# Down projection in seven block products over 16 of 22 key tiles, with the sums of weight blocks made earlier by GpSimd

## The chip, the core and the metric

The kernel runs on one core of a Trainium2 chip. The metric is device time in microseconds (us) of one execution. Engines are called by the profile's names: PE (TensorE matmuls), PEld (its weight loads), DVE (VectorE), ACT (ScalarE), POOL (GpSimd) and SP (SyncE, which here issues nearly all transfers, in one queue in order).

## The reference, cut to what matters

One encoder layer over 1024 tokens of width 1024: a token mixer (mLSTM heads and neighbourhood attention behind one input projection), a cross attention into 256 memory tokens, and a gated feed-forward part with a depthwise convolution, each followed by a layer norm of `alpha * x + f(x)`. Two of its parts matter here: the last matrix product `y @ w_down`, with 22 x 128 = 2816 hidden columns, and the projection of the normed input, out of which the q and k of the mLSTM heads come.

```python
def conv_ffn(x, w_up, b_up, w_dw, b_dw, w_down, b_down):
    h = x @ w_up + b_up
    h = lax.conv_general_dilated(h, w_dw[:, None, :], window_strides=(1,), padding='SAME', ...) + b_dw
    g, u = jnp.split(h, 2, axis=-1)
    y = jax.nn.gelu(g, approximate=False) * u
    return y @ w_down + b_down
...
    z = x @ w_in + b_in                      # in hybrid_mixer: q, k, v, gates, ... of both head groups
...
    h = layer_norm(DN_ALPHA * h + conv_ffn(h, w_up[l], b_up[l], w_dw[l], b_dw[l], w_down[l], b_down[l]),
                   ln3_w[l], ln3_b[l])
```

## The kernel before

All large products are made of f16 pairs: an f32 operand, scaled by a power of two, is split into a high part (ACT, line 203) and a low part (DVE, line 204; both in `split16`), and `mm3` (lines 224 to 226) issues three matmuls, high by high, high by low, low by high. The scale comes from a bound on the operand: an ACT pass with `Abs` and an accumulated sum for weights, then a maximum over partitions by way of TensorE (`amax_all`, lines 182 and 183, tile `mx`) and a few small DVE operations (`pow2`, 174 to 176).

The program is written with a tile scheduler, which sorts the instructions of each engine by a timeline that it simulates itself; `tc.issue_after(x)` keeps an instruction behind another. A tile of a pool with n buffers waits until the last readers of the one n before it are done. Each engine, and SP's queue of transfers, then works strictly in the order so found.

Stages, with rough times in the trace: the memory's keys and values and the input projections (to 254); the q/k units (254 to 340), four blocks of weights by a seven-product scheme (`units_gen`, `cu_prep`: two 512 KB loads at line 458 into `wraw` (two buffers), bounds at 310, splits, four GpSimd sums at 476 to 479, splits of the sums; each product is 48 matmuls of 128x512 in tile `cu`); behind the 14th product `back_gen` (mLSTM state) runs beside them; then mLSTM, column projections, neighbourhood attention, cross attention; the feed-forward loop (850 to 1205), 22 units of seven products each (tile `z`) with the convolution on ACT and DVE and the gated product `y` stored tile by tile to DRAM (`y_d`, line 1715). Beside the loop, `survey_down` loads each of the 22 tiles of `w_down` (512 KB, tile `sv`) and takes its bound on ACT.

The down projection begins inside the last two units: `y_scale(0)` gives the scale of y for the key tiles below `NG` = 18 (the last four have a scale of their own). `y_pair` loads two key tiles of y (1 MB) into one of three rotating raw buffers (`raw8`: two called `two`, one `ur`) and splits them; `w_pair` loads `w_down` by 512 KB into `wraw` and splits it. `dmm` runs `mm3` over key tiles for one of eight token tiles and one of two column halves of 512, in bank tile `dn`. The first column half goes over all token tiles and is kept in `half0`; the second is made token tile by token tile, and each is followed by its norm (`ln_tile`, lines 239 to 258: statistics and products on DVE, a power step on POOL at line 244, a scaling on ACT, an add on POOL at 258) and its store. The residual row `r` is loaded from DRAM (line 1922) and scaled by two POOL passes of 128x1024 (lines 1929 and 1930).

## Time and profile before

| What | Value |
|---|---|
| median of 3 runs | 1470.32 us (1469.87 to 1471.45) |
| profiled execution, its own time | 1471.42 us |
| its span (first to last instruction) | 1469.6 us |
| mean granted TensorE clock | 0.991 |
| busy: PE / DVE / ACT / POOL | 98% / 70% / 56% / 38% |
| matmuls of tile `dn` by line 224, 225 and 226, largest groups | 105 us busy each, no idle time before them |
| transfers | 208.60 MB, mean 142 GB/s |

The span is cut into stretches below: for each engine its busy time. An instruction's row has its start and length in us, the engine, the line (of a helper where one issued it), the operation, what it writes and reads, and in brackets how long its engine had been idle and which instruction released it. A group's row has count, total busy time and mean ns of one, then idle time before and its releasers. Matmuls overlap: their interval is read from one start to the next, not from the length of one.

### The profile page before, as it was taken

What the parts mean: (1) busy time and instruction counts of PE and PEld (TensorE: products, weight loads), DVE (VectorE), ACT (ScalarE), POOL (GpSimd) and SP (SyncE); (2) the same over time, 40 slices, a digit from 0 to 9 for tenths busy, and PEclk for the clock granted to TensorE, in tenths of its full rate; (3) what the DMA queues carried; (4) which work ended last, traced back from release to release, by engine and by line L of the source; (5) the groups of instructions that cost most, each with busy time, mean ns of one, the idle gap of its engine ahead of it and who ended that gap; (6) DMA issues with size and microseconds to landing.
All of it is one profiled execution on the core that took longest, in us unless ns stands there. A gap on an engine that the chain in (4) does not pass through costs nothing.

```text
span 1469.6 us, 21479 instructions
## 1 busy us (share of the span) xinstructions
PE 1435.0 (98%) x7996; PEld 847.4 (58%) x7996; DVE 1031.0 (70%) x1950; ACT 821.9 (56%) x1385; POOL 559.5 (38%) x440
## 2 busy tenths in 40 slices
PE   8999899999999999999999999999999999999998
PEld 6998777456766777774444444444444444444445
DVE  7877866536767787689657778878887879627333
ACT  5765465665454476524455678787777667411010
POOL 4452356502233765145214053544444400302352
PEclk9999999999999999999999999999999999999999
DMA  8855654213554643653443333333334228621111
GB/s 305 308 192 185 188 196 152 94 50 116 162 140 149 222 143 123 245 181 78 92 100 101 118 109 130 146 117 127 117 129 149 96 99 289 228 84 46 58 58 58
DMA packets 116382, 208.60 MB, mean 142 GB/s; under 512 B 40627, under 2 KB 69555, under 8 KB 112950
## 3 DMA queue, kind: packets, MB, share of 16 engines
q1 hardware_dynamic: 115984, 206.47, 42.2%
q8 instruction: 63, 1.03, 0.3%
q0 software_dynamic: 144, 0.49, 0.2%
q14 instruction: 41, 0.34, 0.1%
q10 hardware_dynamic: 150, 0.27, 0.0%
HBM read 154.15 MB, written 45.15 MB: 136 GB/s over the span
## 4 chain that ended last, share of the span: by engine, by line
PE 78%; DVE 7%; DMA 5%; ACT 4%; issue 3%; POOL 2%; SPq 1%; DVEq 0%; ACTq 0%; POOLq 0%
PE z L226 7%; PE z L225 7%; PE z L224 7%; PE dn L224 5%; PE dn L226 5%; PE dn L225 5%; PE S L224 4%; PE S L225 4%; PE S L226 4%; PE tk L225 2%; PE tk L224 2%; PE tk L226 2%; PE cl L224 2%; PE cl L225 2%; PE cl L226 2%
## 5 line engine op out<-in xcount | busy, mean ns | idle before, releaser
L225 PE MATMUL dn<-wlo,yp 128*128 128x512 f16 (+1 forms) x284 | 105.1, 370 | 0.0
L224 PE MATMUL dn<-whi,yp 128*128 128x512 f16 (+1 forms) x284 | 105.0, 370 | 0.0
L226 PE MATMUL dn<-whi,yp 128*128 128x512 f16 (+1 forms) x284 | 104.3, 370 | 0.0
L1708 DVE SCALAR_TENSOR_TENSOR cbuf<-C,wdw,cbuf 128x1024 f32<-128x1024 f32 x44 | 64.9, 1477 | 39.3 <-ACT cbuf L1707 39.3
L226 PEld LDWEIGHTS <-wlo 128*128 128x128 f16 x540 | 52.8, 98 | 56.7 <-DVE wlo L204 1.5
L224 PEld LDWEIGHTS <-whi 128*128 128x128 f16 x540 | 52.8, 98 | 56.1 <-issue 3.2
L225 PEld LDWEIGHTS <-whi 128*128 128x128 f16 x540 | 52.8, 98 | 54.5 <-issue 1.8
L244 POOL TENSOR_TENSOR lnrs<-lnrs,mhalf 128x1 f32<-128x1 f32 x32 | 23.4, 731 | 154.9 <-DVE lnrs L243 148.1
L1566 POOL TENSOR_TENSOR wraw<-two 128x512 f32<-128x512 f32 x15 | 30.1, 2009 | 123.0 <-issue 121.8
L204 DVE SCALAR_TENSOR_TENSOR wlo<-wraw,us,whi 128x1024 f16<-128x1024 f32 (+1 forms) x48 | 61.7, 1305 | 18.6 <-ACT whi L203 18.6
L1709 DVE SCALAR_TENSOR_TENSOR cbuf<-C,wdw,cbuf 128x1024 f32<-128x1024 f32 x44 | 71.3, 1622 | 1.1
L1707 ACT ACTIVATE cbuf<-C,bdw,wdw 128x1024 f32<-128x1024 f32 x44 | 54.2, 1237 | 18.4 <-DVE C L1745 17.7
L203 ACT ACTIVATE whi<-wraw,us 128x1024 f16<-128x1024 f32 (+1 forms) x48 | 51.0, 1103 | 15.3 <-DVE us L176 14.7
L224 PEld LDWEIGHTS <-yp 128*128 128x128 f16 x370 | 36.2, 98 | 39.9
L225 PEld LDWEIGHTS <-yp 128*128 128x128 f16 x370 | 36.2, 98 | 39.8
L226 PEld LDWEIGHTS <-yp 128*128 128x128 f16 x370 | 36.2, 98 | 39.7
L254 ACT ACTIVATE r<-r,lnrs 128x1024 f32<-128x1024 f32 x11 | 13.6, 1238 | 79.3 <-DVE lnrs L253 79.2
L224 PE MATMUL tk<-whi,Bo 128*128 128x256 f16 (+1 forms) x192 | 53.2, 277 | 1.6 <-DVE stage L204 1.6
L224 PE MATMUL tk<-whi,Be 128*128 128x256 f16 (+1 forms) x192 | 52.6, 274 | 0.9 <-DVE stage L204 0.9
L225 PE MATMUL tk<-wlo,Be 128*128 128x256 f16 (+1 forms) x192 | 52.4, 274 | 0.9 <-DVE wlo L204 0.9
L225 PE MATMUL tk<-wlo,Bo 128*128 128x256 f16 (+1 forms) x192 | 53.2, 277 | 0.0
L226 PE MATMUL tk<-whi,Bo 128*128 128x256 f16 (+1 forms) x192 | 53.1, 277 | 0.0
(556 smaller groups left out, 4854.2 us busy)
## 6 DMA issues: line engine op xcount, KB each, us to landing
two<-in_w_up_dram SPq DMA_DIRECT2D x15, 1024.0 KB
sv<-in_w_down_dram SPq DMA_DIRECT2D x22, 512.0 KB
y<-cbuf SPq DMA_DIRECT2D x22, 512.0 KB
wraw<-in_w_down_dram SPq DMA_DIRECT2D x22, 512.0 KB
ur<-in_w_up_dram SPq DMA_DIRECT2D x7, 1024.0 KB
two<-y SPq DMA_DIRECT2D x7, 1024.0 KB
r<-h SPq DMA_DIRECT2D x11, 512.0 KB
wraw<-in_w_tok_dram SPq DMA_DIRECT2D x10, 512.0 KB
```

The costliest lines, as they stand in the source:

```text
L203: A.activation(hi, src, AF.Copy, scale=s)
L204: return V.scalar_tensor_tensor(lo, src, s, hi, op0=OP.mult, op1=OP.subtract)
L224: T.matmul(ps, lh, rh, start=first, stop=False, skip_group_check=skip)
L225: T.matmul(ps, lh, rl, start=False, stop=False, skip_group_check=skip)
L226: return T.matmul(ps, ll, rh, start=False, stop=last, skip_group_check=skip)
L244: G.tensor_tensor(rs[:, 0:1], rs[:, 0:1], mhalf[:, 0:1], OP.pow)
L254: A.activation(r, r, AF.Identity, scale=rs[:, 0:1], bias=rs[:, 1:2])
L1566: G.tensor_tensor(S1, A21, A22, OP.add)
L1707: A.activation(c, C[:, 1:SEQ + 1], AF.Identity, scale=wdw[:, 1, j:j + 1], bias=bdw[:, j:j + 1])
L1708: V.scalar_tensor_tensor(c, C[:, 0:SEQ], wdw[:, 0, j:j + 1], c, op0=OP.mult, op1=OP.add)
L1709: V.scalar_tensor_tensor(c, C[:, 2:SEQ + 2], wdw[:, 2, j:j + 1], c, op0=OP.mult, op1=OP.add)
```

## The change

The down projection takes the key tiles 0 to 15 as 2 x 2 blocks: two halves of the tokens, two halves of the keys (eight tiles each), two halves of the columns. It forms seven products instead of eight: A11B11, A12B21, A22T4, and with sums of blocks n2T2, n1T1, s3T3, n4B22; each is four token tiles by eight key tiles by three matmuls of 128x512. `a_sums` makes the sums of y blocks in the stage (two DVE and two POOL operations of 128x512 for each of eight steps). The products are gathered in `C`, eight tiles of 128x1024, by `into` (ACT copies, DVE adds). The six key tiles 16 to 21 (`NG` = 16) go in a last pass, token tile by token tile, both column halves, each followed by its norm; `rest(n)` has prepared the residual in three POOL passes. All splits of y and `w_down` are made in this stage, from raw buffers of 128x2048 by `raw8`.

The sums of weight blocks T1 to T4 are made beside the q/k units by `td_gen`, in 16 steps at every 1st, 3rd, 5th and 7th product of a unit: a 512 KB load into `draw` (three buffers), the bound by ACT `Abs`, four POOL additions in place, a 512 KB store to `td_d` in DRAM. `survey_down` in the feed-forward loop is left with six of its 22 loads and ACT passes.

```diff
+            def td_gen():
+                ...
+                load(0)
+                load(1)
+                for n in range(16):
+                    raw = raws.pop(n)
+                    with tc.issue_after(taken[0].ins):
+                        A.activation(junk, raw.rearrange("p b c -> p (b c)"), AF.Abs, accum_out=sums[:, NFF + n:NFF + n + 1])
+                    B11, B12, B21, B22 = (raw[:, i] for i in range(4))
+                    G.tensor_tensor(B11, B11, B12, OP.add)
+                    G.tensor_tensor(B12, B12, B22, OP.add)
+                    G.tensor_tensor(B22, B22, B11, OP.add)
+                    G.tensor_tensor(B21, B21, B22, OP.add)
+                    o = n // 2 * 512 + n % 2 * 256
+                    S.dma_start(td_d[:, :, o:o + 256].rearrange("n p c -> p n c"), raw)
+                    load(n + 2)
+                    yield
...
             for n, _ in enumerate(units_gen(cu0)):
+                if n % 7 % 2 == 0:
+                    next(td, None)
                 if n >= 14:
                     next(bg, None)
+            run(td)
             run(bg)
...
-        NG = NFF - 4
+        NG = 16
...
+            def a_sums(i, s):
+                ...
+                V.tensor_tensor(t[:, 0], o, o8, OP.subtract)
+                V.tensor_tensor(t[:, 1], t[:, 0], e, OP.subtract)
+                G.tensor_tensor(u[:, 0], e, o, OP.subtract)
+                G.tensor_tensor(u[:, 1], t[:, 1], e8, OP.add)
+                for m, src in enumerate((t, u)):
+                    h = SH[m][i // 4][:, :, :, i % 4]
+                    split16(h[:, 0], h[:, 1], src, s)
...
+            def b_form(name, home):
+                ...
+                for q in range(2):
+                    raw = raw8()
+                    if name[0] == "B":
+                        S.dma_start(raw.rearrange("p (i c) -> p i c", i=4),
+                                    I["w_dn"][4 * q:4 * q + 4, :, n * 512:n * 512 + 512].rearrange("i p c -> p i c"))
+                    else:
+                        S.dma_start(raw, td_d[n, :, q * 2048:q * 2048 + 2048])
+                    h, l = home[q]
+                    split16(h, l, raw, sd)
...
+            def dprod(banks, a, b, first, js=range(4), outer=False):
+                for j, i in [(j, i) for i in range(8) for j in js] if outer else [(j, i) for j in js for i in range(8)]:
+                    t = slice(j * 128, j * 128 + 128)
+                    h, l = a[i]
+                    mm3(banks[j], h[:, t], l[:, t], *BF_[b][i], first and i == 0, i == 7, skip=True)
...
+            b_form("B11" ...); a_plain("A11" ...); b_form("B21" ...); a_plain("A12" ...); b_form("T4" ...); a_plain("A22" ...)
+            dprod(Z4, A12, "B21", True)
+            b_form("T2", kept["H0"])
+            for i in range(4):
+                a_sums(i, s1)
+            dprod(Z4, A22, "T4", True)
+            b_form("T1", YH)
+            for i in range(4, 8):
+                a_sums(i, s1)
+            dprod(X4, n2, "T2", False, outer=True)
+            b_form("T3", H1)
+            dprod(W4, n1, "T1", True, outer=True)
+            b_form("B22", kept["H0"])
+            dprod(X4, s3, "T3", False, outer=True)
+            order = [4, 5, 6, 7, 0, 1, 2, 3]
+            def rest(n):
+                tt, r = order[n], wp.tile([128, WP], F32, name="wraw", tag="wraw", bufs=2)[:, :D]
+                S.dma_start(r, h2_d[tt * 128:(tt + 1) * 128, :])
                 G.tensor_tensor(r, r, rw, OP.mult)
                 G.tensor_tensor(r, r, rb, OP.add)
+                G.tensor_tensor(C[tt], C[tt], r, OP.add)
...
+            for tt in order:
+                r = C[tt]
+                for a, n in ((0, 512), (512, 256), (768, 256)) if last else ((0, 512), (512, 512)):
+                    p = bank("dn")[:, :n]
+                    for f in range(NG, NFF):
+                        mm3(p, ys[f][0][:, t0], ys[f][1][:, t0], wl[f][0][:, a:a + n], wl[f][1][:, a:a + n], ...)
+                    V.scalar_tensor_tensor(r[:, a:a + n], p, ratio, r[:, a:a + n], op0=OP.mult, op1=OP.add)
                 ln_tile(r, lw, lb, small, late=last, eps=ep, parts=2 if last else 1, pieces=4 if last else 2)
```

Lines of the changed file are higher by one from line 200 on, and more from 990 on. The order shows the rest. SP's queue at the third and fourth q/k unit, before: the loads of `w_cu` (the last two are the fourth unit's) follow one another.

```order
L828 DMA mo<-ev 128x256 x3
L930 DMA mo<-mo 128x512 x2
L458 DMA wraw<-in_w_cu_dram 128x1024 x4
L916 DMA whi<-mrow 128x512 x2
L948 DMA wraw<-in_w_col_dram 128x1024
```

And now:

```order
L931 DMA mo<-mo 128x512 x2
L459 DMA wraw<-in_w_cu_dram 128x1024 x2
L1006 DMA td<-draw 128x4x256
L991 DMA draw<-in_w_dn_dram 128x4x256
L1006 DMA td<-draw 128x4x256 x2
L991 DMA draw<-in_w_dn_dram 128x4x256
L459 DMA wraw<-in_w_cu_dram 128x1024
L991 DMA draw<-in_w_dn_dram 128x4x256
L459 DMA wraw<-in_w_cu_dram 128x1024
L1006 DMA td<-draw 128x4x256
L991 DMA draw<-in_w_dn_dram 128x4x256
```

Three stores of sums (`td<-draw`, of steps 0 to 2) and four loads of `draw` now stand ahead of the last `w_cu` load; the load in the last row is that of step 6, behind the store of step 3. The first three `draw` loads stand far ahead, in the 13th place of SP's queue at the program's start.

ACT at the split of the fourth unit, before:

```order
L310 ACTIVATE whi,l_3511<-wraw 128x1024
L505 ACTIVATE q_3217<-cu,bsc,us 128x2x128
L505 ACTIVATE q_3219<-cu,bsc,us 128x2x128
L505 ACTIVATE k_3218<-cu,bsc,us 128x2x128
L505 ACTIVATE k_3220<-cu,bsc,us 128x2x128
L203 ACTIVATE whi<-wraw,us 128x512
L203 ACTIVATE whi<-wraw,us 128x1024
L203 ACTIVATE whi<-ev_3620,us 128x512
```

And now:

```order
L311 ACTIVATE whi,l_3584<-wraw 128x1024
L506 ACTIVATE q_3218<-cu,bsc,us 128x2x128
L506 ACTIVATE q_3220<-cu,bsc,us 128x2x128
L999 ACTIVATE djunk,sums<-draw 128x1024
L506 ACTIVATE k_3219<-cu,bsc,us 128x2x128
L506 ACTIVATE k_3221<-cu,bsc,us 128x2x128
L204 ACTIVATE whi<-wraw,us 128x512
L999 ACTIVATE djunk,sums<-draw 128x1024
L204 ACTIVATE whi<-wraw,us 128x1024
L204 ACTIVATE whi<-ev_3709,us 128x512
```

The bound of step 5 (first L999) stands ahead of the unit's split, that of step 6 (second L999) between its first two pieces.

POOL beside the last token tiles' norms, now (`lnrs` is the power step of a norm, `L259` the last add of a norm, `L2010` to `L2012` the passes of `rest`):

```order
L245 TENSOR_TENSOR lnrs<-lnrs,mhalf 128x1
L2010 TENSOR_TENSOR wraw<-wraw,vec_12595 128x1024 x2
L2011 TENSOR_TENSOR wraw<-wraw,vec_12597 128x1024
L259 TENSOR_TENSOR D_12146<-D_12146,ur 128x1024
L2011 TENSOR_TENSOR wraw<-wraw,vec_12597 128x1024
L245 TENSOR_TENSOR lnrs<-lnrs,mhalf 128x1
L2012 TENSOR_TENSOR D_12144<-D_12144,wraw 128x1024
L2012 TENSOR_TENSOR D_12145<-D_12145,wraw 128x1024
L245 TENSOR_TENSOR lnrs<-lnrs,mhalf 128x1
```

Four passes of `rest` and one add stand between the first tile's power step and the second's, two more passes ahead of the third's. Before, two passes of 128x1024 and one add stood between one tile's power step and the next one's.

242 lines of the change are left out of this document (128 added, 114 removed).

## The prediction

> **What bounds the kernel now.** I read the busy shares first, then the windows of the stages that the change touches, then the waits there, and the chain of waits last.
>
> ```profile
> PE 1435.0 (98%) x7996; PEld 847.4 (58%) x7996; DVE 1031.0 (70%) x1950; ACT 821.9 (56%) x1385; POOL 559.5 (38%) x440
> PE 78%; DVE 7%; DMA 5%; ACT 4%; issue 3%; POOL 2%; SPq 1%; DVEq 0%; ACTq 0%; POOLq 0%
> ```
>
> ```profile
> 250.00:300.00 50.00, 48.33 (x247) 24.35 (x245) 29.08 (x64) 30.64 (x56) 22.15 (x19) 1.00 0.32 110
> 300.00:350.00 50.00, 49.12 (x290) 30.62 (x289) 23.80 (x71) 33.87 (x90) 8.11 (x9) 1.00 0.35 96
> 1000.00:1050.00 50.00, 50.00 (x235) 22.73 (x234) 40.01 (x47) 38.21 (x48) 23.67 (x12) 1.00 0.34 127
> 1200.00:1250.00 50.00, 50.00 (x235) 23.03 (x234) 44.84 (x51) 39.48 (x44) 0.00 (x0) 1.00 0.68 228
> 1300.00:1350.00 50.00, 50.00 (x234) 22.84 (x233) 28.20 (x34) 8.64 (x8) 10.18 (x4) 1.00 0.19 64
> 1400.00:1450.00 50.00, 50.00 (x234) 22.65 (x232) 18.55 (x33) 3.72 (x3) 21.08 (x11) 1.00 0.17 64
> ```
>
> The columns after the window's length are busy time (and count) of PE, its weight loads, DVE, ACT, POOL, then the granted clock, the DMA share and GB/s. In the feed-forward loop (1000) and in the down projection (1205 to 1462) TensorE is busy for all 50 us of each window at full clock: a matmul less there is its whole interval less. In the q/k units it lacks 1.7 and 0.9 us of 50, so it is nearly the bound there too, but with something close behind it. Their first product and the last start at:
>
> ```profile
> 253.83 0.38 PE L224 MATMUL cu<-Be,whi 128*128 128x512 f16 x1
> 337.98 0.38 PE L224 MATMUL cu<-TX1h,whi 128*128 128x512 f16 x1
> ```
>
> **The change, part by part.**
>
> *Fewer products.* Before, 8 token tiles x 22 key tiles x 2 column halves x 3 matmuls = 1056 of 128x512. Now 7 products x 96 = 672, and 8 x 6 x 2 x 3 = 288 for the six tiles left, 960 together. The interval:
>
> ```profile
> 1099.79 0.38 PE L226 MATMUL z<-TX1l,unitYl 128*128 128x512 f16 x1
> 1101.08 0.38 PE L226 MATMUL z<-TX1l,unitYl 128*128 128x512 f16 x1
> ```
>
> Six matmuls take 1.29 us, 0.215 each (the windows' 234 in 50 us say 0.214): 96 x 0.215 = **-20.6 us**, if TensorE stays dense.
>
> *Whether it stays dense.* The stage takes in 34 transfers of 1 MB into three rotating raw buffers, where 11 such and 22 of half the size stood before, and splits all but the eight of the row sums at the full 128x2048. The prices:
>
> ```profile
> 1205.55 2.19 ACT L203 ACTIVATE yp<-two,sc 128x1024 f16<-128x1024 f32 x2 [2.19 <-DVE sc L176]
> L203 ACT ACTIVATE yp<-two,sc 128x1024 f16<-128x1024 f32 x14 | 15.2, 1137 | 9.6 <-DVE sc L176 9.0 <-PE z L226 0.7
> L204 DVE SCALAR_TENSOR_TENSOR yp<-two,sc,yp 128x1024 f16<-128x1024 f32 x14 | 17.5, 1280 | 0.2 <-ACT yp L203 0.2
> L938 DVE TENSOR_TENSOR whi<-whi,G 128x512 f32<-128x512 f32 x16 | 10.2, 678 | 0.0
> L1932 DVE TENSOR_TENSOR r<-r,half 128x512 f32<-128x512 f32 x4 | 5.1, 1275 | 1.8 <-POOL r L1930 1.8
> 1370.97 0.34 SPq L1945 DMA_DIRECT2D out_dram<-r  x1
> 1373.65 0.32 SPq L1922 DMA_DIRECT2D r<-h  x1
> 1377.11 2.36 POOL L1929 TENSOR_TENSOR r<-r,vec 128x1024 f32<-128x1024 f32 x1 [6.17 <-DMA r<-h]
> ```
>
> A raw is split in 2 x 1.14 us on ACT and 2 x 1.28 on DVE behind it. DVE's sum over the seven products (151 us of TensorE): 34 x 2.56 = 87, two subtractions for each of eight row sums = 11, sixteen adds of bank halves = 11, 109 together, 72%. So DVE has room. A buffer's round is its load, then the split, about 3.8 until DVE is done. 512 KB need 3.46 us from issue to use (1373.65 to 1377.11); at the 228 GB/s of the window at 1200 another 512 KB adds 2.3, so 5.8 + 3.8 = 9.6 us, and 34 such in three buffers are 109 us, again under 151. I cost the density at 0; the cover is this difference of some 42 us, and if it is gone TensorE waits for the overhang (a rival below). The first split waits, as before, for the scale (at 1205.55), and TensorE has the last unit's products to do meanwhile.
>
> *The end.* GpSimd now does three passes of 128x1024 for each token tile (two before), the last twelve of them in its queue among the last tiles' norms, and each row load waits for one of two buffers.
>
> ```profile
> L1930 POOL TENSOR_TENSOR r<-r,vec 128x1024 f32<-128x1024 f32 x4 | 11.3, 2844 | 0.1
> L258 POOL TENSOR_TENSOR wraw<-wraw,yp 128x1024 f32<-128x1024 f32 x3 | 7.4, 2475 | 7.7 <-DVE wraw L257 7.7
> L1941 DVE TENSOR_TENSOR r<-r,dn 128x512 f32<-128x512 f32 x4 | 2.8, 689 | 26.6 <-PE dn L226 26.6
> 1462.37 0.43 DVE wraw L1941
> ```
>
> A token tile's matmuls now come every 36 x 0.215 = 7.8 us. The second tile's power step stands behind five of these passes (5 x 2.5 = 12 us) plus a load of 3.5, so I estimate it some 7 us late. DVE waits there in order, and a tile costs it about 5 us, so it catches up about 2.8 us on each of six tiles. Best case 0; worst, nothing caught up: 7. I take **+2.5**, nearer to the catching up. What follows the last matmul stays about 7.5 us (1462 to 1469.6).
>
> *Weight sums beside the q/k units.* Sixteen steps: one ACT pass (1.06 + 0.19, as in the rows at 287.71 and 288.68), four GpSimd adds of 128x256, a store, a load. GpSimd was 30 us busy in these 100 (the first two windows), DMA 0.33: by totals, 16 x 4 x 0.67 = 43 us of GpSimd and 16 MB fit. What doesn't is the order. The rows of before around the fourth unit:
>
> ```profile
> 281.21 1.90 SPq L458 DMA_DIRECT2D wraw<-in_w_cu_dram  x2
> 287.71 1.06 ACT L310 ACTIVATE whi<-wraw 128x1024 bf16<-128x1024 f32 x1
> 288.68 0.19 ACT L310 ACTIVATION_READ_ACCUMULATOR whi<-wraw 128x1 f32 x1
> 287.76 1.27 POOL L476 TENSOR_TENSOR ev<-wraw 128x512 f32<-128x512 f32 x1 [1.26 <-DMA wraw<-in_w_cu_dram]
> 298.29 0.29 DVE L183 TENSOR_REDUCE us<-mx 128x1 f32<-128x128 f32 x1 [1.86 <-PE mx L182]
> 299.18 1.76 ACT L203 ACTIVATE whi<-wraw,us 128x512 f16<-128x512 f32 x2
> 300.85 1.32 ACT L203 ACTIVATE whi<-ev,us 128x512 f16<-128x512 f32 x2
> PE cu L226 <- DVE wlo L204: 0.8, 1, 0.8
> 290.00:300.00 10.00, 10.00 (x50) 4.86 (x48) 3.57 (x12) 1.84 (x4) 1.65 (x2) 1.00 0.07 23
> L736 POOL TENSOR_TENSOR tsum<-Bo 128x256 f32<-128x256 f16 x8 | 5.4, 674 | 0.0
> L739 POOL TENSOR_TENSOR tsum<-Bo,tsum 128x256 f32<-128x256 f16 x8 | 7.6, 946 | 0.0
> ```
>
> Its last two weight loads are issued at 281 to 283 and are there at 285.0 and 287.7; now stores of three steps' sums, each waiting for GpSimd, stand ahead of them in SP's queue, so I put them at about 290. That alone is harmless, since the split waits for the maximum at 298.3. But the ACT pass of step 6 now stands between the first piece of that split (299.18) and the rest, and it needs a load that waits for the third step's store to have landed, whose last add stands on GpSimd behind the fourth unit's own four adds. GpSimd from 290: four of 1.27 and five of 0.67 to 0.95, about 9.2, is 299; the store 2.7 (1370.97 to 1373.65, from a store to the load that reuses its buffer), the load 3.46, the pass 1.25: 306.6, against 299.9 before for that piece. TensorE had no slack there (it waited 0.8 us for this split), so it stops some 7 us; best case 4 (loads on time), worst 12. A stop brings the half clock:
>
> ```profile
> 25.55 1.09 PE L612 MATMUL tp<-ident,x 128*128 128x128 f32 x8 [0.29 <-POOL x L258]
> 30.13 0.58 PE L226 MATMUL mem<-memTh,wlo 128*128 128x256 f32 x1 [3.49 <-DVE wlo L577]
> 36.27 0.33 PE L224 MATMUL mem<-memTh,whi 128*128 128x256 f32 x1
> ```
>
> After 3.5 us idle the intervals are half speed from 30.1 to 36.3, which loses 3.1 us. At other places it may be shorter, so I take 2 to 3: **+9** in all (0 if the order does not bite, 15). By the Trainium skill, "TensorE: Matmul & The Clock Gate", Part 1, full clock returns after about 3.4 us of sustained work. That would make the loss 1.7 us and the sum 1 us lower; the row's 6.1 us of half clock says more. After this step the chain goes on at 11 to 12 us for each buffer's round, and ends about with the shifted units, so I add nothing.
>
> *The start.* The first three loads of the sums (1.5 MB) have no producer and stand 13th in SP's queue, among the loads of the first 25 us.
>
> ```profile
> 5.00:15.00 10.00, 10.00 (x26) 6.12 (x25) 7.91 (x9) 7.80 (x9) 3.11 (x1) 1.00 1.02 408
> 15.00:25.00 10.00, 10.00 (x84) 10.00 (x83) 8.88 (x20) 4.50 (x7) 5.41 (x4) 1.00 1.03 413
> ```
>
> DMA is full there: 1.5 MB at 410 GB/s are 3.8 us for whatever stands behind. TensorE already waits for weights at 30, but that wait ends on splits, not on a load. I take **+1.5**, between -1 (another order) and +5.
>
> *The loop.* Sixteen ACT passes of 1.2 us and 8 MB of loads leave the feed-forward loop: TensorE is dense there at ACT 38 of 50, so 0.
>
> Sum: -20.6 + 2.5 + 9 + 1.5 = **-7.6 us**. The profiled execution took 1471.42 us with a span of 1469.6, which makes a span of 1462.0 and a time of 1463.8; the median run, 1470.32, is 1.1 us below the profiled one, so **1462.7 us**.
>
> **Rivals.**
>
> *The sums ride free.* If the fourth unit's loads keep their place and step 6 comes in time, the +9 is gone: 1453.7. For it: GpSimd is busy only 1.65 us between 290 and 300, so the third step's adds have room if they come ahead of the unit's own. Against: store, load and pass follow the last of these adds by 7.4 us, so it must be done by 292.5, some 2.5 us after the loads at 290.
>
> *The sums set the pace* (the slower side). Sixteen steps through three buffers are 5.3 rounds; the 84 us between the units' first product and their last allow 15.8 us a round. My round is 1.24 + 2.7 to 3.8 + 2.7 + 3.46 = 10 to 11 us alone. From 15.8 on, each ACT pass holds ACT's queue, and the units with it. At 19 us a round the units take 101 us, +17 more in place of the catch-up and beside the one stop: -20.6 + 2.5 + 17 + 9 + 1.5 = +9.4, 1479.7. It ends slower than before once a round is over 17.3 us. For it: an add waits on GpSimd behind units' adds, and a pass on ACT behind splits. Against: GpSimd is under half full.
>
> *The down stage starves.* A buffer's round over 151 x 3 / 34 = 13.3 us makes the raws the bound. DVE operations with two inputs beside GpSimd take 1.28 us where 0.68 is normal (the L1932 row against L938). In the Trainium skill, "GPSIMD Engine Reference", Specifications, GpSimd shares VectorE's SBUF interface and contends with its two-input operations; the L1932 row agrees, and the rule speaks against row sums shared by both engines. At 14.3 us a round: 34 x 14.3 / 3 = 162, 11 us of waits, so 1473.7. Against it: GpSimd works for only some 20 to 30 us of these 151.
>
> **How the numbers follow.** Chances: the forecast 0.45, free 0.22, pace 0.13, starving 0.15, others 0.05. The forecast's own range is 1456 to 1470. The range of 8 in 10 takes in the free sums and half of the two slower cases: 1450 to 1476. A measurement here tells 0.2% (2.9 us) from no change. Faster: 0.39 out of the forecast's 0.45, all of the free sums and 0.03 of the rest, 0.64; same: 0.06 of the forecast's and 0.08 of the others, 0.14; slower: what is left, 0.22.
>
> **What would show it.** Right: 960 columns' worth of matmuls after about 1212, TensorE at 50 of 50 in windows up to the end; one wait for a split (DVE wlo) of 5 to 10 us in the last q/k unit, then half clock; a wait for the power step on DVE near the second of the last token tiles. Wrong: TensorE's idle time spread over the products with DMA as releaser; long waits of ACT's L999 for a load, one for each step; several us more before 60 us.

## The result, and the profile after

| | before | after |
|---|---|---|
| median, us | 1470.37 (1469.87 to 1471.45) | 1486.13 (1485.82 to 1486.89) |
| ratio, 95% interval | | 1.0107 [1.0089, 1.0124] |
| profiled span, us | 1469.6 | 1483.4 |
| first q/k product (tile `cu`) | 253.8 | 262.0 |
| from there to the first mLSTM product (tile `num`) | 93.5 | 112.5 |
| from there to the first feed-forward product (tile `z`) | 479.2 | 478.9 |
| from there to the last matmul | 635.6 | 619.4 |
| from there to the end | 7.5 | 10.6 |

The change made the kernel 1.07% slower. The spans differ by 13.8 us, and the table splits them: the start +8.2, the q/k units +19.0, the middle -0.3, the loop and the down projection -16.2, the end +3.1. The rows behind it, of after (a group's row gives count, the least, median and largest length in ns, and the first and last start):

```profile
L225 PE MATMUL cu<-Be,whi x32: 379/379/634, 262.0 to 354.2; 128*128 128x512 f16 x32
L1041 PE MATMUL num<-V,whi x128: 272/275/377, 374.5 to 487.4; 128*128 128x129 f32 x128
```

and its last matmul:

```profile
1472.79 0.27 PE L227 MATMUL dn<-whi,wlo 128*128 128x256 f16 x1
```

The windows of after, columns as in the prediction:

```profile
300.00:350.00 50.00, 35.44 (x181) 19.09 (x178) 16.30 (x38) 31.44 (x71) 30.52 (x38) 0.90 0.62 199
1250.00:1300.00 50.00, 50.00 (x233) 22.70 (x232) 41.99 (x31) 33.32 (x29) 5.48 (x3) 1.00 0.67 242
1300.00:1350.00 50.00, 45.65 (x212) 20.47 (x210) 46.89 (x39) 26.23 (x23) 28.10 (x16) 1.00 0.70 250
1400.00:1450.00 50.00, 50.00 (x234) 22.65 (x233) 19.27 (x30) 3.72 (x3) 47.68 (x23) 1.00 0.16 53
```

Three things are to be seen. From 300 to 350 PE has 35.44 us of 50 where it had 49.12, though ACT (31.44), DVE (16.30) and POOL (30.52) are not full either: something waits for an order, not for capacity. From 1300 to 1350 PE has 45.65, and there DVE is nearly full (46.89). From 1400 on POOL is nearly full (47.68, before 21.08). What PE waited for between 250 and 380, the three longest (us in total, times, longest):

```profile
PE cu L225 <- ACT whi L204: 8.4, 1, 8.4
PE cu L225 <- ACT k L506: 2.9, 1, 2.9
PE tp L867 <- ACT kw L871: 2.2, 1, 2.2
```

The stop of 8.4 us can be followed back row by row. First SP's queue (start, length, line, transfer):

```profile
284.49 0.60 SPq L991 DMA_DIRECT2D draw<-in_w_dn_dram  x1
290.33 4.30 SPq L1006 DMA_DIRECT2D td<-draw  x2
294.74 0.60 SPq L991 DMA_DIRECT2D draw<-in_w_dn_dram  x1
295.45 0.83 SPq L459 DMA_DIRECT2D wraw<-in_w_cu_dram  x1
297.54 0.56 SPq L991 DMA_DIRECT2D draw<-in_w_dn_dram  x1
298.19 0.57 SPq L459 DMA_DIRECT2D wraw<-in_w_cu_dram  x1
310.92 0.38 SPq L1006 DMA_DIRECT2D td<-draw  x1
313.89 0.56 SPq L991 DMA_DIRECT2D draw<-in_w_dn_dram  x1
```

Then POOL, ACT and PE over the same time (in brackets the idle time before, and what ended it):

```profile
293.19 1.06 POOL L1004 TENSOR_TENSOR draw<-draw 128x256 f32<-128x256 f32 x1
301.80 1.26 POOL L478 TENSOR_TENSOR hm<-wraw 128x512 f32<-128x512 f32 x1 [7.55 <-DMA wraw<-in_w_cu_dram]
310.18 0.72 POOL L1004 TENSOR_TENSOR draw<-draw 128x256 f32<-128x256 f32 x1
301.69 1.06 ACT L311 ACTIVATE whi<-wraw 128x1024 bf16<-128x1024 f32 x1 [6.92 <-DMA wraw<-in_w_cu_dram]
318.18 1.06 ACT L999 ACTIVATE djunk<-draw 128x1024 bf16<-128x1024 f32 x1 [7.17 <-DMA draw<-in_w_dn_dram]
319.24 1.13 ACT L204 ACTIVATE whi<-wraw,us 128x1024 f16<-128x1024 f32 x1
321.04 0.61 PE L225 MATMUL cu<-TX1l,whi 128*128 128x512 f16 x1 [8.44 <-ACT whi L204]
```

Two stores wait for POOL's adds until 294.2. Behind them in the queue stand the fourth unit's own weights, which go out at 295.45 and 298.19 (the second one after a `draw` load that waits for a store to land). ACT and POOL, each in order, wait some 7 us for these weights, with `draw` passes and adds queued behind. So the adds end at 310.9; the store, the next load (313.89) and the pass (318.18) follow; and the rest of the fourth unit's split stands behind that pass. The `draw` buffer loaded at 284.49 is loaded again at 313.89: 29.4 us for this round. All sixteen passes run from 270.6 to 371.6 (the row is below), which is 101.0 x 3 / 15 = 20.2 us a round on average.

Where in the stage the 19.0 us are lost is read from the 336 matmuls of tile `cu`. (28 products make 336, so a product is twelve matmuls: four key tiles, three matmuls each. The 48 named with the kernel before is wrong.) The table counts how far PE is behind the kernel before, from the first of them on:

| matmul of `cu` | before, start | after, start | behind, us |
|---|---|---|---|
| 1st | 253.83 | 261.98 | 0 |
| 157th | 290.10 | 298.17 | -0.1 |
| 181st | 295.27 | 306.38 | 3.0 |
| 205th (behind the stop) | 301.61 | 321.04 | 11.3 |
| 241st | 312.98 | 334.70 | 13.6 |
| 313th | 332.73 | 358.73 | 17.9 |
| first of `num` | 347.3 | 374.5 | 19.0 |

Two of these rows, of before and then of after:

```profile
290.10 0.38 PE L224 MATMUL cu<-Be,whi 128*128 128x512 f16 x1
312.98 0.38 PE L224 MATMUL cu<-Bo,whi 128*128 128x512 f16 x1
```

```profile
298.17 0.38 PE L225 MATMUL cu<-Be,whi 128*128 128x512 f16 x1
334.70 0.38 PE L225 MATMUL cu<-Bo,whi 128*128 128x512 f16 x1
```

Up to 298 nothing is lost, though four of the sixteen passes have run by then (the fourth starts at 293.62). The wait for the late weights costs 3.0 us; the stop of 8.4, a wait of 1.1 and the half clock behind them cost 10.6; another 5.4 are lost after that, where ACT still waits for `draw` loads (5.85 us ahead of the pass at 344.90). So the loss comes as a few stops, not as a slower pace of the whole stage. The whole stage, before and then after:

```profile
253.80:347.30 93.50, 90.95 (x476) 48.86 (x475) 48.73 (x115) 59.51 (x133) 25.57 (x22) 1.00 0.30 89
```

```profile
262.00:374.50 112.50, 95.93 (x481) 50.44 (x478) 55.63 (x117) 74.40 (x160) 72.44 (x82) 0.94 0.63 200
```

PE is idle 16.6 us where it was idle 2.6, and its matmuls take 5.0 us more at a mean clock of 0.94.

### The profile page after: what moved, and what is told of

Its sections match the earlier page's. It is cut to its first block, busy times and chain, and to the rows that moved or that the text cites. A ratio compares the mean times of both kernels' runs of the same rounds, so it can differ in the third digit from the quotient of the medians.

```text
span 1483.4 us, 21399 instructions
## 1 busy us (share of the span) xinstructions
PE 1420.7 (96%) x7864; PEld 835.2 (56%) x7864; DVE 1074.7 (72%) x1956; ACT 850.9 (57%) x1399; POOL 655.3 (44%) x528
## 5 line engine op out<-in xcount | busy, mean ns | idle before, releaser
L225 PEld LDWEIGHTS <-whi 128*128 128x128 f16 x574 | 56.5, 98 | 68.8 <-ACT whi L204 8.7
L226 PEld LDWEIGHTS <-whi 128*128 128x128 f16 x574 | 56.5, 98 | 62.5 <-issue 7.2
L227 PEld LDWEIGHTS <-wlo 128*128 128x128 f16 x574 | 56.4, 98 | 61.7 <-DVE wlo L205 2.0
L1600 POOL TENSOR_TENSOR wraw<-two 128x512 f32<-128x512 f32 x15 | 30.1, 2008 | 123.0 <-issue 121.8
L204 ACT ACTIVATE whi<-wraw,us 128x1024 f16<-128x1024 f32 (+1 forms) x48 | 51.1, 1103 | 10.8 <-DVE us L177 10.3
L225 PE MATMUL tk<-whi,Be 128*128 128x256 f16 (+1 forms) x192 | 52.6, 274 | 0.8 <-ACT whi L204 0.5
L227 PE MATMUL tk<-whi,Be 128*128 128x256 f16 (+1 forms) x192 | 52.6, 274 | 0.0
L225 PE MATMUL S<-kq,h1T 128*128 128x512 f16 x128 | 48.6, 379 | 0.0
L226 PE MATMUL S<-kq,h1T 128*128 128x512 f16 x128 | 48.5, 379 | 0.0
L227 PE MATMUL S<-kq,h1T 128*128 128x512 f16 x128 | 48.5, 379 | 0.0
L1821 POOL TENSOR_TENSOR wraw<-two 128x512 f32<-128x512 f32 x2 | 3.8, 1885 | 97.2 <-DMA two<-y 92.5
L1270 ACT ACTIVATE P<-P,mn 128x256 f32<-128x256 f32 (+1 forms) x64 | 35.7, 558 | 16.0 <-DVE mn L1268 14.9
L255 ACT ACTIVATE D<-D,lnrs 128x1024 f32<-128x1024 f32 x5 | 6.2, 1241 | 66.2 <-DVE lnrs L254 66.2
```

The lines of the kernel that those rows point to most:

```text
L204: A.activation(hi, src, AF.Copy, scale=s)
L225: T.matmul(ps, lh, rh, start=first, stop=False, skip_group_check=skip)
L226: T.matmul(ps, lh, rl, start=False, stop=False, skip_group_check=skip)
L227: return T.matmul(ps, ll, rh, start=False, stop=last, skip_group_check=skip)
L255: A.activation(r, r, AF.Identity, scale=rs[:, 0:1], bias=rs[:, 1:2])
L1270: A.activation(P[:, :nk], P[:, :nk], AF.Exp, scale=-1.0, bias=mn[:, 0:1], accum_out=mn[:, 1:2])
```

## The experiments

All are edits of the changed kernel, timed against the kernel before. "q/k" is from the first `cu` product to the first `num` product, "loop, down" from the first `z` product to the last matmul, both in us of the profiled run. These lengths are of one execution of each: e10's took 1487.38 us in all (its median is 1483.16), e14's 1459.95 (median 1462.07). Kernels that do the same in the loop and the down projection differ there by up to 3 us (e12 617.2, e6 620.2), so less than that in this column shows nothing. e4, e9, e13 and e14 leave the sums out and so do less than the whole work.

| run | median | ratio [95%] | first `cu` | q/k | loop, down | end |
|---|---|---|---|---|---|---|
| before | 1470.37 | 1 | 253.8 | 93.5 | 635.6 | 7.5 |
| after | 1486.13 | 1.0107 [1.0089, 1.0124] | 262.0 | 112.5 | 619.4 | 10.6 |
| e1_late_draw | 1474.69 | 1.0022 [1.0009, 1.0035] | 251.5 | 110.7 | 618.8 | 10.7 |
| e2_no_abs | 1467.11 | 0.9964 [0.9951, 0.9977] | 261.1 | 92.5 | 617.3 | 9.9 |
| e4_no_sums | 1456.90 | 0.9898 [0.9881, 0.9914] | 254.3 | 92.8 | 620.3 | 10.0 |
| e5_loop | 1480.90 | 1.0060 [1.0040, 1.0079] | 252.9 | 93.0 | 643.0 | 9.9 |
| e6_late_no_abs | 1476.42 | 1.0036 [1.0023, 1.0048] | 255.9 | 110.4 | 620.2 | 10.1 |
| e7_sums_dve | 1473.35 | 1.0016 [1.0005, 1.0027] | 255.5 | 110.4 | 618.5 | 8.0 |
| e8_rest_dve | 1480.26 | 1.0058 [1.0041, 1.0076] | 253.8 | 110.2 | 620.1 | 11.6 |
| e9_bounds_only | 1455.64 | 0.9895 [0.9882, 0.9908] | 252.4 | 92.5 | 619.0 | 9.8 |
| e10_gp_stores | 1483.16 | 1.0084 [1.0070, 1.0099] | 257.5 | 107.9 | 620.0 | 10.0 |
| e11_loop3 | 1476.47 | 1.0034 [1.0020, 1.0047] | 252.9 | 93.4 | 640.1 | 10.0 |
| e12_gp_queue | 1481.19 | 1.0078 [1.0066, 1.0091] | 252.8 | 117.9 | 617.2 | 9.9 |
| e13_no_stores | 1464.29 | 0.9958 [0.9944, 0.9972] | 252.5 | 100.9 | 618.7 | 10.3 |
| e14_no_adds | 1462.07 | 0.9947 [0.9931, 0.9963] | 251.4 | 98.8 | 618.5 | 9.8 |
| e15_early | 1464.69 | 0.9961 [0.9946, 0.9976] | 262.0 | 93.2 | 618.2 | 10.3 |
| e16_split | 1459.70 | 0.9919 [0.9905, 0.9933] | 252.6 | 92.5 | 623.8 | 10.2 |
| e17_tail | 1459.48 | 0.9923 [0.9910, 0.9935] | 251.3 | 92.5 | 623.9 | 11.2 |

### The parts one by one

**e1_late_draw**: the loads of the sums wait until the first load of `w_cu` has been issued.

```
-                        S.dma_start(raws[n], I["w_dn"][n // 2]...)
+                        with tc.issue_after(taken[1].ins):     # the first load of w_cu
+                            S.dma_start(raws[n], I["w_dn"][n // 2]...)
```

> The changed kernel with one thing different: the first three loads of the weight sums wait in SP's queue for the first load of the q/k units, so they leave the first 25 us; the rest of the order stays. Theory (the 1.5 MB push back the loads behind them in a full DMA): the memory's matmuls end near 112 us again instead of 118.5, and the first q/k product starts near 255 instead of 262, so 1486.1 - 7 = 1479 (1476 to 1481). Rival (the start lost time because the order of other engines changed, or because of noise): the q/k units still start after 260 and the time stays within 2 us of 1486.

The first `cu` product starts at 251.5, 10.5 us earlier than in after, and the median falls by 11.4 us. So three early loads of 512 KB cost all of the lost start (and more than was expected: 1474.69 lies below the range). Whether by their transfers alone, or also by the other order that the scheduler then gave to ACT, this run does not separate. What they delay, in after: they go out at 13.01, and loads that the splits need stand behind them.

```profile
13.01 3.04 SPq L991 DMA_DIRECT2D draw<-in_w_dn_dram  x3
16.83 3.17 SPq L329 DMA_DIRECT2D cr<-in_w_tok_dram  x1
20.10 1.72 SPq L572 DMA_DIRECT2D wr<-in_w_xk_dram  x3
```

A wait of PE and a window that follow:

```profile
PE mem L225 <- ACT whi L577: 1.9, 2, 1.4
```

```profile
30.00:40.00 10.00, 6.67 (x29) 5.96 (x30) 6.44 (x10) 6.81 (x10) 5.92 (x4) 0.67 0.64 229
```

Before, the `cr` load went out at 12.72 and the three `wr` loads from 14.59; the window from 20 to 30 had a DMA share of 0.70, not 1.06, and PE had 9.87 us from 30 to 40, not 6.67. The loads come 4 to 5.5 us later. ACT's splits of `wr`, which started at 24.52, 32.77 and 34.29, now start in a row from 35.86, behind a norm's scaling and another split in its order. PE waits for them and falls back to half clock a second time (0.85 in the window at 40, before 1.00). The memory's matmuls end 6.5 us later (118.8 against 112.3). The other 1.7 of the 8.2 us are lost between 150 and 170 us, and why is open; e4, which has no early loads, is 1.5 us late there too.

**e2_no_abs**: no ACT pass beside the units; the bounds of all 22 tiles are taken in the feed-forward loop, as before the change.

```
-                        A.activation(junk, raw..., AF.Abs, accum_out=sums[...])
```

> The changed kernel without the ACT passes beside the q/k units: the bounds of the 16 half tiles are taken in the feed-forward loop as in the kernel before (22 loads and passes there), while loads, GpSimd sums and stores beside the units stay. Theory (the ACT pass of step 6 holds the split of the fourth unit): TensorE's stop of 8.4 us at 321 and its half clock behind it go, while the 2.9 us stop for late weights may stay: 1486.1 - 11 = 1475 (1472 to 1478). Rival (SP's queue holds the unit's weight loads and that is the loss): a stop of 5 us or more stays in that unit and the time is 1482 or more.

This run missed its question. The ACT pass was also what tied a step to the units: without it the scheduler drew the whole chain to the time from 13 to 172 us; from 100 to 160 GpSimd was then busy 16.5 to 19.8 us of each 20. The q/k units lose nothing (92.5), but the start still loses 7 us (first `cu` at 261.1). The time is below both of the expected ranges.

**e4_no_sums**: no `td_gen`; the blocks of sums are loaded as plain blocks of `w_down` instead, so this run leaves the sums out; the bounds of all 22 tiles are taken in the loop.

```
-                        S.dma_start(raw, td_d[n, :, q * 2048:q * 2048 + 2048])
+                        S.dma_start(raw..., I["w_dn"][4 * q:4 * q + 4, :, n * 512:n * 512 + 512]...)
-                    next(td, None)
```

> The changed kernel without the 16 steps beside the q/k units (no load, bound, sum or store there); the four products with sums of weight blocks take plain blocks of w_down in their place, and the bounds are taken in the loop as before. So the block scheme of the down projection is alone. Theory (start and q/k units lost about 27 us, and the down stage with its end gains about 13): 1486.1 - 27 = 1459 (1456 to 1462), with the same 4 us of TensorE waits in the down stage. Rival (the down stage was disturbed by what came before, or the shift of the whole program costs by itself): above 1464.

1456.90 against 1471.03 of the kernel before in this comparison, so the new down projection by itself is worth 14.1 us. Start and q/k units are as before. All that made the kernel slower is in making the sums, 29 us in after (1486.13 less 1456.90).

**e6_late_no_abs**: e1 and e2 together, so that the chain stays beside the units, without ACT passes.

> e1 and e2 together: the first three loads wait for the first load of the q/k units, and the bounds are taken in the feed-forward loop, so that loads, GpSimd sums and stores run from about 225 to 300 with no ACT pass among them. Theory (of the 27 us lost before the down stage, 8 to 10 are the early loads and 17 to 19 the ACT passes that wait for loads): the q/k units take 93 us from their first product to the first matmul of the state as in the kernel before, and the time is about 1458 (1455 to 1461), 12 us faster than the kernel before. Rival (stores and loads of the sums in SP's queue, ahead of the units' weights, cost by themselves): stops of 3 us or more for late weights in the units or in the token projection, 1464 or more.

The q/k units take 110.4 us with no pass of ACT in them, against 110.7 in e1. So the pass in the middle of a split, by which I had explained the stop, is not what the loss hangs on: without it as much is lost, at other places (10.4 us by the 157th matmul of `cu`, 6.2 more between the 181st and the 205th). Its waits between 250 and 380:

```profile
PE stb L879 <- ACT kw L872: 5.2, 1, 5.2
PE mx L183 <- DVE l L313: 5.0, 1, 5.0
ACT whi L311 <- DMA wraw<-in_w_cu_dram: 16.1, 4, 9.6
```

and two rows of its SP queue:

```profile
310.08 0.36 SPq L1005 DMA_DIRECT2D td<-draw  x1
310.53 0.46 SPq L459 DMA_DIRECT2D wraw<-in_w_cu_dram  x1
```

Here the fourth unit's weights go out at 310.53, behind stores that wait for adds: the same wait, passed on by SP's queue instead of ACT's.

**e10_gp_stores** and **e12_gp_queue**: other queues for the transfers. e10 is e1 with the stores in GpSimd's queue of transfers; e12 is e6 with loads and stores in it, the first loads behind GpSimd's sums of the first unit.

```
-                    S.dma_start(td_d[...], raw)
+                    G.dma_start(td_d[...], raw)
```

> e1 (late first loads, ACT passes beside the units kept) with the 16 stores of the sums issued in GpSimd's own queue behind their last add, so that in SP's queue nothing waits for an add any more, only draw loads that wait for a landed store. Theory A (stores that wait for GpSimd hold the units' weight loads in SP's queue): the fourth unit's weights land in time, TensorE's stops of 2.6 and 8.4 us shrink to 4 together or less, the units take at most 100 us to the first matmul of the state (110.7 in e1), and the time is 1459 to 1465. Theory B (the round of a buffer, through the landed store, is too long for the ACT pass that waits for its load): a stop of 5 us or more behind an ACT pass stays, the units take 105 us or more, the time is 1468 or more.

> e6 (no ACT passes beside the units, bounds in the loop) with loads and stores of the sums both in GpSimd's queue, the first loads behind the sums of the first unit. SP's queue then holds nothing of the sums. Theory (e6's 17 us are SP's queue alone): the units take 93 to 97 us and the time is 1457 to 1462. Rival (GpSimd's waits for landed stores make the units' own sums late): stops for a unit's split of 3 us or more, 1465 or more.

Neither helps. In e10 PE's waits for the fourth unit's split go (2.0 us the longest), a wait of 5.9 us for ACT's `kw` comes in the stage, and more of the loss moves behind it: ACT's passes, which now run on to 375.5, wait 23.0 us for `draw` loads, and PE waits for the ACT work queued behind them; the stretch from the first `num` to the first `z` product, 478.9 in after, is 489.9 here.

```profile
PE num L1043 <- ACT hm L1055: 6.7, 1, 6.7
```

The idle time of ACT ahead of its passes (releaser, us in all, times):

```profile
  DMA draw<-in_w_dn_dram: 23.0, 6
```

In e12 SP's queue is clear of the sums, but the unit's weights still come late: `wraw` is free only when GpSimd's sums of the unit have read it, and these stand behind stores and adds in GpSimd's own order. Issuing a transfer is also work for GpSimd here, 0.77 us each (12.4 us for the 16 stores, 10.0 for 13 loads), so e12 adds a cost of its own and is no clean test of the queue. PE waits 11.2 us at once:

```profile
PE cu L225 <- ACT k L507: 13.0, 2, 11.2
ACT whi L311 <- DMA wraw<-in_w_cu_dram: 14.4, 5, 7.6
```

### How long a round may be

**e9_bounds_only**, **e13_no_stores**, **e14_no_adds**: e1 with less in each round. e9 has only loads and ACT passes; e13 has the adds too but no stores; e14 has the stores but no adds. None of them makes the sums for the down projection (e14 stores the plain blocks).

```
e9, e14:  -  G.tensor_tensor(B11, B11, B12, OP.add)  ...  (four adds)
e9, e13:  -  S.dma_start(td_d[...], raw)
```

> The changed kernel with late first loads (e1), with the 16 loads and ACT passes beside the q/k units, but without the GpSimd additions and without the stores; plain blocks of w_down stand in for the sums later. Theory (an ACT pass costs TensorE only by waiting for a load that waits for sums and a landed store): with loads that wait for the pass three steps before alone, TensorE's stop of 8.4 us goes, and the units lose at most 3 us: 1456 to 1460. Rival (16 ACT passes of 1.25 us are too many beside the units' splits): the units lose 8 us or more, 1465 or more.

> e1 without the 16 stores: loads, ACT passes and GpSimd additions beside the units stay, and plain blocks of w_down stand in for the sums later. A buffer is free again after its last add. Theory A (GpSimd's adds, in one order with the units' own sums, make the loss): the units still take 102 us or more from their first product to the first matmul of the state, the time is 1465 or more. Theory B (the stores do: SP's queue waits for adds, and a buffer for its store): the units take 97 us or less, the time is 1455 to 1460.

> e1 without the 64 GpSimd additions: loads, ACT passes and stores stay (the blocks stored are not sums). A store waits for the ACT pass alone. Theory A (the adds make the loss): the units take 97 us or less and the time is 1455 to 1461. Theory B (the stores in SP's queue, and buffers that wait for a landed store, make it even without adds): 102 us or more, 1465 or more.

The first and last pass of each gives the length of a round: that of after, then that of e9, which differ in nothing but what a round holds and the start.

```profile
L999 ACT ACTIVATE djunk<-draw x16: 1039/1052/1058, 270.6 to 371.6; 128x1024 bf16<-128x1024 f32 x16
```

```profile
L1001 ACT ACTIVATE djunk<-draw x16: 1042/1053/1092, 258.3 to 341.9; 128x1024 bf16<-128x1024 f32 x16
```

| run | a round holds | round, us | behind at 157th, us | at 241st | at 313th | q/k, us |
|---|---|---|---|---|---|---|
| e9 | load, pass | 16.7 | -1.9 | -1.1 | -0.9 | 92.5 |
| e14 | load, pass, store | 18.1 | 3.2 | 4.0 | 4.2 | 98.8 |
| e13 | load, pass, adds | 18.4 | -1.9 | 7.2 | 7.4 | 100.9 |
| e1 | load, pass, adds, store | 20.3 | -1.9 | 11.8 | 13.4 | 110.7 |
| after | the same, early first loads | 20.2 | -0.1 | 13.6 | 17.9 | 112.5 |

Round is (last start - first start) x 3 / 15; "behind" is counted as in the table of the result, from each run's own first `cu` matmul; a minus is ahead of the kernel before. The mean round is no measure of its own. The passes are strung along the units, so their 15 / 3 = 5 rounds last about as long as the stage, and that each us of a round goes with 5 us of the stage, (110.7 - 92.5) / (20.3 - 16.7) = 5.1, is this sum and shows no cause. What shows it is what each run leaves out. Loads and passes alone lose nothing (e9). Without stores 8.4 us of loss remain, without adds 6.3, with both 18.2: neither is the cause alone, and together they cost more than the two by themselves (14.7). The medians say the same (1455.64, 1464.29, 1462.07, 1474.69). Both theories of e13 and of e14 missed their bounds. Each loss stands at one or two places: e14's before the 157th matmul, most of e13's at the stop in front of the 241st.

### Other places for the sums

**e5_loop**, **e11_loop3**: the steps are made in the feed-forward loop, in `survey_down`'s own two tiles `sv` (e5), or in three with the stores in GpSimd's queue (e11).

```
-                if n % 7 % 2 == 0:
-                    next(td, None)
                 A.activation(junk..., t, AF.Abs, accum_out=dsum[:, i:i + 1])     # survey_down, step i
+                if i < 16:
+                    B11, B12, B21, B22 = (t[:, 256 * b:256 * b + 256] for b in range(4))
+                    ...                                                          # four adds, a store
```

> The changed kernel with the 16 steps moved from the q/k units into the feed-forward loop, in place of its 16 loads and bounds there: load, ACT pass, four GpSimd adds in the same tile, store. Theory (GpSimd has half of each window free there and TensorE is dense): nothing is lost in the loop, 1459 (1456 to 1463), faster than the kernel before by some 11 us. Rival (GpSimd's adds come ahead of the unit's own sums, each 2 us beside DVE, and SP's stores ahead of the unit's loads): waits for a unit's weights appear in the loop and the time is 1467 or more.

> e5 (the 16 steps in the feed-forward loop) with three tiles in turn in place of two, and the stores in GpSimd's own queue. Theory (the 20 us that e5 lost in the loop are SP and ACT waiting for a store and for the load behind it): no stop of TensorE over 2.5 us is left in the loop, it takes 418 us from its first product to the down stage as in e4, and the time is 1456 to 1461, 11 us faster than the kernel before. Rival (GpSimd itself is too late for the units' sums, since each of its operations beside DVE takes 1.3 to 2.3 us): ACT's take of a unit waits again, 1466 or more.

The q/k units are free again, and the loop loses instead: 643.0 and 640.1 against 619.4. In e5:

```profile
PE z L225 <- ACT C L1768: 17.0, 5, 5.9
ACT sv L1787 <- DMA sv<-in_w_dr_dram: 23.3, 5, 6.1
```

ACT's bound of a tile waits up to 6.1 us for a load that waits for a store, and the ACT copies that free PE's banks stand behind it. The loads waited for are those of the six tiles that are only surveyed (`in_w_dr_dram`); in e5 such a tile is loaded right behind a step that uses the same buffer. A third tile doesn't change that (e11: 25.9 us of waits for `sv` loads, 11.5 us of PE's for copies).

**e15_early**: without ACT passes, the steps from about 90 to 215 us, anchored behind a load of the projections' weights.

> e2 (no ACT passes among the steps, bounds taken in the feed-forward loop) with the first three loads behind the last of the early weight surveys, at about 90 us, so that the 16 steps run from 90 to 215 us, before the q/k units. Theory (the loss is the steps' place: the first 25 us, where DMA is full, and the units, where GpSimd, ACT and SP are all waited for): the start and the units are those of the kernel without the sums, and the time is 1457 to 1462, faster than the kernel before by 8 us or more. Rival (the steps get in the way of the token projection too, by GpSimd's or SP's order): 1466 or more.

The units are free (93.2), but the stage from 90 to 215 loses what they had lost: the first `cu` product is at 262.0, PE waits 6.5 us for a DVE step (before 1.7), and ACT 21.9 us for GpSimd's sums of that stage (before 6.5). The time lies between theory and rival.

**e16_split**: the bounds stay beside the q/k units, as in e9; the sums are made in the loop from a second load of each tile, in three tiles, stored by GpSimd's queue, with no ACT pass there.

```
                 # td_gen: loads and Abs passes alone, loads behind the first load of w_cu
-                    G.tensor_tensor(B11, B11, B12, OP.add)   # ... four adds, the store
                 # survey_down, 22 steps:
+                if i >= 16:
+                    A.activation(t, t, AF.Abs, accum_out=dsum[:, i:i + 1])
+                else:
+                    ...                                       # four adds
+                    G.dma_start(td_d[...], t...)
```

> The two halves of a step are taken apart: loads and ACT bounds stay beside the q/k units, with late first loads (as in e9, which lost nothing), and the GpSimd sums with a second load and the store are made in the feed-forward loop, three tiles in turn, stores in GpSimd's queue, with no ACT pass on them (e11 without its 16 ACT passes). The result is the full one. Theory (a step costs only where an engine in order waits on a round of load, pass, sums and store that is longer than its pace): nothing waits for these sums before the down stage, so the loop takes 417 us from its first product as in e4, and the time is 1455 to 1461, some 12 us faster than the kernel before. Rival (GpSimd's adds beside DVE make the unit's own sums late, or stretch DVE): TensorE stops in the loop, 1465 or more.

1459.70, ratio 0.9919 [0.9905, 0.9933]: faster than both kernels, and inside the expected range. Start and q/k units lose nothing. The loop and the down projection give back some 5 us against e9 (623.8 to 619.0), of which PE's waits for copies are 2.8 in two groups (in e9 0.3); the rest is not traced. The larger group:

```profile
PE z L225 <- ACT C L1769: 1.5, 3, 1.0
```

### The down projection and the end

**e7_sums_dve** and **e8_rest_dve**, both on e6 (1476.42): e7 makes all sums of y blocks on DVE, e8 the third pass of `rest` on DVE for the last four tiles.

```
e7: -  G.tensor_tensor(u[:, 0], e, o, OP.subtract);  G.tensor_tensor(u[:, 1], t[:, 1], e8, OP.add)
    +  V.tensor_tensor(u[:, 0], e, o, OP.subtract);  V.tensor_tensor(u[:, 1], t[:, 1], e8, OP.add)
e8: -  G.tensor_tensor(C[tt], C[tt], r, OP.add)
    +  (V if n > 3 else G).tensor_tensor(C[tt], C[tt], r, OP.add)
```

> e6 with all four operations of each sum of y blocks on DVE (two of four were GpSimd's). Theory (GpSimd beside DVE stretches DVE's operations, 0.68 to 1.75 and 2.35 to 3.35 us in the rows after, and that makes the 2 to 4 us of TensorE waits in the third and fourth product): DVE's added 16 x 0.68 = 11 us are paid back by the stretch of some 15 us that goes, and the time is that of e6 within 2 us. Rival (DVE's own load is what makes it late): the waits in the down stage grow to 8 us or more and the time rises by 5 us or more.

> e6 with the last pass of the residual (the add to the gathered products) on DVE for the last four token tiles. Theory of the prediction (GpSimd's passes delay the power steps and the backlog reaches the end): the time from TensorE's last matmul to the end falls from 10 to about 7.5 us. Rival (the backlog is made up by the end, and the 2.5 us are the norm of the last tile but one, which stands on DVE ahead of the last tile's statistics since tiles now follow every 7.8 us): the end stays at 10 us, though DVE's waits for the power step fall from 13.8 us in sum to below 6.

The window of the row sums, 50 us, of e6 and then of e7 (1.4 us earlier there, as its loop is):

```profile
1290.00:1340.00 50.00, 46.76 (x209) 20.55 (x207) 46.19 (x42) 25.39 (x23) 27.83 (x15) 0.97 0.64 230
```

```profile
1288.60:1338.60 50.00, 47.85 (x216) 21.40 (x215) 46.77 (x57) 25.07 (x23) 0.00 (x0) 0.97 0.67 246
```

DVE does fifteen operations more in this window of e7 and is only 0.6 us busier: the same work takes it less time when GpSimd is quiet. The four splits of 128x2048 beside the row sums take 2.34, 2.80, 3.36 and 3.36 us in e6, and 2.34 to 2.35 each in e7. The median falls by 3.1 us, which neither side expected. That the matmuls gain by it (620.2 to 618.5) is not shown: the difference is within that of equal stages, and PE still waits 2.1 us for a row sum (2.2 in e6). The gain that is seen is at the end, 10.1 to 8.0. In e8 the end grew, to 11.6, which neither side expected; its median is 3.8 us above that of e6, in runs that overlap (1475.02 to 1484.43 and 1471.17 to 1481.77). Both ends are read from POOL's power steps. In after the last two of them, with a pair of DVE operations between:

```profile
1471.08 0.55 POOL L245 TENSOR_TENSOR lnrs<-lnrs,mhalf 128x1 f32<-128x1 f32 x1 [0.18 <-DVE lnrs L244]
1477.23 1.41 DVE L251 SCALAR_TENSOR_TENSOR D<-D,lnmv,vec 128x512 f32<-128x512 f32 x2
1477.46 0.92 POOL L245 TENSOR_TENSOR lnrs<-lnrs,mhalf 128x1 f32<-128x1 f32 x1 [0.62 <-DVE lnrs L244]
```

The second to seventh power steps start at 1440.98, 1447.11, 1453.45, 1459.17, 1465.12 and 1471.08, about 6.0 us apart, where PE makes a tile every 7.74. The last matmul of the second tile is at 1472.79 - 6 x 7.74 = 1426.4; before, the last power step followed its last matmul by 1.9 (1462.06 to 1463.94). So the second tile is 12.7 us late, each tile wins back about 1.7, and the last one is still 2.8 late (1477.46 against 1472.79 + 1.9): that is the longer end. In e7 the second step stood 34.1 us ahead of the last matmul, not 31.8 as in after, and the end was 2.6 shorter. In e8 DVE waited 6.6 us for power steps, not 13.5, but did the four passes itself, and the delay stayed (its second step stood 31.5 us ahead).

**e17_tail** (on e16): the product of the last tile but one with the norm's weight (L258) goes from DVE to GpSimd.

```
-        a = V.tensor_tensor(r, r, w_t, OP.mult)
+        a = (G if gm else V).tensor_tensor(r, r, w_t, OP.mult)     # gm: tt == order[-2]
```

> e16 with the last tile but one's product of its norm (128x1024) on GpSimd in place of DVE. Theory (the end takes 10 us after the last matmul, not 7.5, because this product stands on DVE ahead of the last tile's statistics): the end falls to 8 to 8.7 us and the time by 1 to 2 us against e16. Rival (the end is set by something else): it stays at 10 us.

Missed: 1459.48 against 1459.70, no difference, and the end took 11.2 us. The last tile's statistics come earlier (L251 starts 2.3 us after the last matmul, in after 4.4), but this pair ran beside GpSimd:

```profile
1448.92 3.49 DVE L251 SCALAR_TENSOR_TENSOR D<-D,lnmv,vec 128x512 f32<-128x512 f32 x2
1449.09 2.77 POOL L259 TENSOR_TENSOR D<-D,ur 128x1024 f32<-128x1024 f32 x1
```

The pair at L251 took 3.49 us where it takes 1.41 in after (1477.23), and the power step stood behind POOL's passes.

## Why the prediction was wrong

The forecast was 1462.7 us, with a range to 1476; the kernel took 1486.13. Against the predicted -7.6 of the sum stand +13.8 in the profiled runs. Three terms were too good by 10.0 (the units), 6.7 (the start) and 4.4 us (the products).

- *Weight sums beside the q/k units*, the term that failed most: +19.0 for +9. The stop came where it was put, in the fourth unit between the pieces of its split and behind the pass of step 6, and with its half clock it cost 10.6 us, near the 9. Two other steps failed. "I put them at about 290. That alone is harmless" was wrong: the fourth unit's weights were issued at 295.45 and 298.19, and the wait for them cost 3.0 us. "After this step the chain goes on at 11 to 12 us for each buffer's round, ... so I add nothing" was wrong too: ACT waited on for `draw` loads, and 5.4 us more were lost. A round was 20.2 us on average, and 29.4 for the one around the stop. My 10 to 11 us summed a round's own parts; what it waits for in the queues of ACT (third unit's splits and copies until 293.6), POOL and SP is as long again. Taking out adds and stores takes all of the loss away (e9), taking out the ACT pass (e6) or moving transfers to another queue (e10, e12) does not.
- The rival *The sums set the pace*, to which I gave 0.13, had the direction and the waits that it named, but not the course: at its 5.3 rounds, 20.2 us each would have cost 23 us beside the stop, and 19.0 were lost in all, none of them in the first half of the matmuls. Its counter-argument, "GpSimd is under half full", was not even true: POOL was busy 30.52 of 50, and my own totals of 30 and 43 us in 100 had said so. It would have been no argument anyway, since PE stopped with no other engine full.
- The rivals *ride free* and *starves* fell: no free sums, and the raws of the down projection were no bound (PE 50.00 of 50 at 1250).
- *The start*: +8.2 for +1.5, past the upper end of 5. The transfer time (1.5 MB, 3.8 us) was about right as a delay of the loads (4 to 5.5 us). The step that failed is "that wait ends on splits, not on a load": the wait at 30 is the same as before (3.5 us), but the splits behind it came later, and PE waited again and had half clock a second time. e1 shows that the early loads are the cause.
- *Fewer products* and *whether it stays dense*: -16.2 for -20.6. 4.35 us are missing in the window at 1300. The count of DVE work was not the error (672 matmuls at 0.215 are 144.5 us and not 151, which makes DVE's share 75% for 72%) but its price beside GpSimd. PE waits for the low half of a row sum, and (second row: count, least, median and largest ns) a raw's DVE split takes up to 3.35 us there where 2.35 is the least:

```profile
PE dx L227 <- DVE SX2l L205: 3.9, 2, 2.2
```

```profile
L205 DVE SCALAR_TENSOR_TENSOR wlo<-two,sc,whi x3: 2346/2352/3353, 1279.7 to 1341.8; 128x2048 f16<-128x2048 f32 x3
```

The prediction had this contention as a reason for a rival, by a row of before and by the Trainium skill, "GPSIMD Engine Reference", Specifications, on the shared SBUF interface. The rule agrees with e7 (3.36 against 2.35 us) and e17 (3.49 against 1.41). I had counted it only against the buffers' round, not against DVE's own load, and I had misread its price: the mean of 1.28 us in the L1932 row mixes two operations alone (0.68 and 0.69) with two beside a GpSimd pass (1.58 and 2.15). The row of before (least, median and largest ns):

```profile
L1932 DVE TENSOR_TENSOR r<-r,half x4: 677/1134/2154, 1338.4 to 1415.7; 128x512 f32<-128x512 f32 x4
```

- *The end*: +3.1 for +2.5, right by luck, with two errors that cancel. The power step of the second tile was 12.7 us late, not 7, since POOL did three passes for a tile from further behind (47.68 us of 50 busy). A tile costs DVE 6.0 us with its waits for ACT and POOL, not 5, so it wins back 1.7 us and not 2.8, and 2.8 us of delay were left at the last matmul. By the prediction's own 7 and 2.8 nothing would have been left after three tiles; the 2.5 was a guess between its two ends.
- *The loop*: as predicted, 0. PE's waits in the loop are the same ones as before (2.3 and 0.4 us for `TX1l` and `TX1h`).
- Half clock behind the stop: the matmuls at 321.04 run at half speed and full speed is back at 326.2, with one more idle time of 1.1 us within, so about 4.1 us of matmuls ran at half speed and some 2 us were lost by it, as put down (2 to 3). By the Trainium skill, "TensorE: Matmul & The Clock Gate", Part 1, it takes about 3.4 us of sustained work. From 323.20 on it took 3.0, so here the page was nearer than the row of 6.1 us that I preferred.
